# Small products of the HGRN heads and the state-space branch, cut in pieces and placed between the k steps of the projections

## The chip, the cores and the metric

The kernel runs on one core of one Trainium2 chip. The metric is the device time of one execution in microseconds, the median of several runs. Half a dozen engines work side by side: TensorE (matrix products; its weight loads are listed apart), VectorE, ScalarE, GpSimd, and SyncE, which only issues transfers. Transfers run on DMA engines.

## The reference, cut to what matters

The program is two transformer-like blocks on a sequence of 512 tokens and 1024 features, in float32. The change lies in the mixer of the second block, where 16 extra tokens stand ahead of the sequence (528 in all):

```
p   = rmsnorm(h) @ w_in                       # 1024 -> 7 x 1024
y_a = s5_mixer(p[:, :1024])                   # state-space branch: 64 groups of 16
y_b = hgrn2_mixer(q, f, i, og)                # p[:, 1024:5120]: 8 heads of 128
out = sigmoid(g1) * (y_a @ Wa) + sigmoid(g2) * (y_b @ Wb)      # gates: p[:, 5120:]

# one HGRN head, chunk by chunk:
#   o     = mask(q_in @ k_in.T) @ v + q_in @ state
#   state = decay * state + k_out.T @ v
#   o     = rmsnorm(o) * g * silu(og)
# state-space branch: states by a linear recurrence over time, y = C @ states + D * u
```

## The kernel before, in words

Every large product is done in three passes (`mm3`, lines 122 to 128): both operands are split into a high and a low part, and high x high, high x low and low x high are summed in one PSUM bank. A projection of the second block is `prod2` (line 1110): 128 output features of all tokens, in two column ranges of 264 or 258 tokens, eight k steps for each; a k step is the three passes of one 128-row slice of the contraction. So a projection has 16 k steps, 48 products on TensorE, and it fills a PSUM tile of two banks, of which there are two. The small products take PSUM tiles of one bank (`aux`), of which there are four. Weights come through landing buffers (`raw`, line 86: two, and a third one in this stage, in turn), are split by ScalarE and VectorE (lines 131, 132) into one of three slots, and stay there until their products are done.

The stage of this document runs from about 866 to 1302.8 us. Head by head (`head`, line 1250) come four projections: forget gate f, output gate og, input i, query q, and between them long chains on ScalarE and VectorE that make the scaled keys (line 1297 the last of them) and queries (line 1303). The back half of a head is small products in plain float32, which appear as two records each: transposes of i and of the output keys (1311, 1315); the scores within chunks, 4 x 4 products with 32 streamed columns each (1328) and one for the extra tokens (1334); the key-value products for the states (1339, 1341); the outputs (1351, 1352, 1354); and, after a norm on VectorE (1365), transposes back (1371, 1373).

The state-space branch has three parts. Its input is written to DRAM and read back in another layout as U (line 1175). `s5_state` makes the driving terms in eleven groups of small products with 64 by 66 columns (1195), then runs the recurrence on VectorE, 64 dependent steps of four instructions (1206 to 1209). `s5_out` rearranges the states on ScalarE (1216), then makes the outputs in ten groups of up to seven (1228, 1229; 66 columns), each group with its own loaded matrices (1224), then a gelu (1232), and y goes to DRAM (1234) and is read back (1426) for the gated output.

`gates` (line 1385) are 16 more projections after the eight heads, with a sigmoid and a store of each by GpSimd (1395).

What sets the order: the functions are generators, and a loop (from line 1398) steps through them by hand, one head's projections in turn with the former head's back half and, from head 4 on, a group of state-space outputs. That is the order of tracing. A planner in the language's layer then orders each engine's instructions by its own estimate of when they are ready; among those that are ready, the one traced first goes first. Once planned the order of an engine is fixed, and each engine works in that order; so does each queue that issues transfers (SyncE for the loads, GpSimd for most stores).

Of the kernel before, what the change touches and what calls it, by code (L numbers as in the profile page):

```python
# [69 lines left out]
class Kern:  # L70
# [15 lines left out]
    def raw(self):  # L86
        """The next landing place of a weight load."""
        self.nraw += 1
        if self.xraw is not None and self.nraw % 3 == 2:
            return self.xraw.tile([P, WCAP], F32, tag="xraw", bufs=1, name=self.nm("xraw"))  # L90
        return self.wpool.tile([P, WCAP], F32, tag="wraw", bufs=self.wbufs[0], name=self.nm("wraw"))
# [12 lines left out]
    def split_w(self, H, L, raw, sz):  # L104
        """H, L <- the two parts of raw, in two pieces so that neither engine is held for long."""
        h = sz // 2
        for a, b in ((0, h), (h, sz)):
            self.split(H[:, a:b], L[:, a:b], raw[:, a:b])

    def load_w2(self, srcs, kt, n):  # L110
        """Several [kt*128, n] blocks in one weight slot."""
# [28 lines left out]
    def rsqrt_act(self, out, ss, n, tag):  # L140
        """out <- (ss / n + EPS) ** -0.5: square root, reciprocal, one Newton step."""
# [11 lines left out]
    def rsqrt_dve(self, out, ss, n, tag):  # L153
        """out <- (ss / n + EPS) ** -0.5 by a bit estimate and three Newton steps."""
# [14 lines left out]
    def later(self, lag, fn):  # L169
        """Queue fn to be traced after the next lag products."""  # L170
# [96 lines left out]
    def ada_tiles(self, c0, n, dst, acc):  # L267
        """dst <- columns c0.. of silu(c) @ w_ada + b_ada, one column per 128; a generator of its steps."""
# [16 lines left out]
    def bcast_rows(self, dst, rstd, n):  # L285
        """dst [P, n*128] <- rstd[:, t] of token t*128+p, on every partition."""
# [8 lines left out]
    def sumsq_add(self, kt, acc, sq, x, e=None):  # L295
        """acc <- acc + x * x, feature tile by feature tile."""
# [7 lines left out]
    def sumsq_rows(self, ps, acc, t0, sizes):  # L304
        """Per token sums over the partitions of acc: column t0 + i of ps for the i-th token tile."""
# [5 lines left out]
    def rstd_rows(self, ps, cols, rb):  # L311
        """rb, on every partition: the reciprocal roots of the mean squares of the tokens in cols; ps: their sums of squares."""
# [17 lines left out]
    def scale_split(self, H, L, x, g):  # L330
        """H, L <- the two parts of x * g, g per partition."""
# [3 lines left out]
    def modulate(self, tiles, src, rb, G, sh, H, L):  # L335
        """H, L <- the two parts of src * rb * G + sh, feature tile by feature tile."""
# [52 lines left out]
    def rope(self, out, x, key, t, heads, rstd):  # L389
        """out, x: [P, heads, d] views; rstd [P, heads]."""  # L390
# [13 lines left out]
    def scores(self, qT, kT, mask):  # L404
        """qT, kT: [d, 512] (scaled). Softmax rows of the four query tiles."""
# [22 lines left out]
    def probs_T(self, probs):  # L428
        """Per key tile j: the probabilities of queries j*128.., keys on the partitions."""
# [21 lines left out]
    def block1(self):  # L451
        nc, tc, A = self.nc, self.tc, self.A
        V = self.V = {}
        with ExitStack() as es:
            b1 = es.enter_context(tc.tile_pool(name="b1", bufs=1, reuse_waits="tile"))
            # x in, its transpose, and the first modulation columns
# [8 lines left out]
            with tc.tile_pool(name="b1x", bufs=1, reuse_waits="tile") as xp:  # L465
# [6 lines left out]
                # silu(c) @ w_ada for the first shift and scale: the last rows on the tensor engine  # L472
# [63 lines left out]
            # latents  # L536
# [56 lines left out]
            # MLA q: 2 x 4 heads of 96  # L593
# [33 lines left out]
            # MLA k, v: 2 x 4 heads of 128  # L627
# [29 lines left out]
            # dilated q, k, v  # L657
# [34 lines left out]
            # attention  # L692
# [60 lines left out]
            for kh in range(2):  # L753
                if kh:
                    # x2 * G2 for the first products, which run before the token norms are known
# [34 lines left out]
        # FFN  # L790
# [100 lines left out]
    def expm1_parts(self, pool, x, parts, n):  # L891
        """2^k and expm1(r) with x = k ln2 + r."""
# [82 lines left out]
    def s5_poles_T(self):  # L975
        """The poles' powers with the states on the partitions, in both halves."""
# [133 lines left out]
    def prod2(self, W, fs, src, ranges, nk=KD):  # L1110
        """T-layout product: PSUM [P, 2, 512]; ranges: two (start, n) column ranges of src."""
        ps = self.psP.tile([P, 2, 512], F32, tag="pp", bufs=2, name=self.nm("pp"))
        for a, (c0, n) in enumerate(ranges):
            for kt in range(nk):
                self.mm3(ps[:, a, :n], (W[0][:, kt, fs], W[1][:, kt, fs]), (src[0][:, kt, c0 : c0 + n], src[1][:, kt, c0 : c0 + n]), kt == 0, kt == nk - 1)
        return ps[:, :, : ranges[0][1]]

    def block2(self):
# [17 lines left out]
        # hgrn lower bounds: softmax over the two rows, first row  # L1136
# [42 lines left out]
        def s5_state():  # L1179
            nonlocal Hs  # L1180
            v_ = slot(2).rearrange("p a b -> p (a b)").rearrange("p (c r g) -> p c r g", c=66, r=2)
            for c0 in range(0, 32, 3):
# [13 lines left out]
                nc.scalar.copy(v_[:, :, :, c0 : c0 + n].rearrange("p c r g -> p r g c"), p4)  # L1196
            self.tap("v", v_)
# [13 lines left out]
        def s5_out():  # L1211
# [8 lines left out]
            for g0 in range(0, 64, 7):  # L1220
                yield
                n = min(7, 64 - g0)
                MO = self.raw().rearrange("p (g s x) -> p g s x", s=2, x=P)
                nc.sync.dma_start(MO[:, :n].rearrange("p g s x -> p g (s x)"), self.MO_d[:, g0 : g0 + n])
                ps = self.aux()
                for i in range(n):
                    o = ps[:, i * 66 : i * 66 + 66]
# [22 lines left out]
        def head(hd, Ws, fs):  # L1250
# [6 lines left out]
            yield  # L1257
# [4 lines left out]
            yield  # L1262
# [42 lines left out]
            Q1, QI = E1, E3  # L1305
            yield
            # token-layout v and k_out
            def tok(src, s):
                pt_ = self.aux()
                for c in range(NT):  # L1310
                    nc.tensor.transpose(pt_[:, c * P : c * P + P], ch(src)[:, c], self.ident)
                o = T(s, 1, (P, NT, P))
# [5 lines left out]
                return o, om  # L1318
            VT, VM = tok(I, "VT")
            KT, KM = tok(KO, "KT")  # L1320
# [3 lines left out]
            for c in range(NT):  # L1324
                for i in range(4):
                    n = 32 * (i + 1)
                    lhs = KX[i][:, c] if i else ch(K1)[:, c, :32]
                    nc.tensor.matmul(p3[:n, c, 32 * i : 32 * i + 32], lhsT=lhs, rhs=ch(Q1)[:, c, 32 * i : 32 * i + 32], start=True, stop=True)  # L1328
            for i in range(4):
# [6 lines left out]
            # states before each chunk  # L1336
# [3 lines left out]
            for c in range(3):  # L1340
# [305 lines left out]
```

## Time and profile before

| | |
|---|---|
| median of 3 runs | 1876.71 us (1876.2 to 1882.28) |
| the profiled execution, first to last instruction (span) | 1874.8 us |
| TensorE busy, share of the span | 96% |
| VectorE | 58% |
| ScalarE | 42% |
| GpSimd | 17% |
| stage of the heads and gates | 866 to 1302.8 us |

The profiled execution's own time is known by its span alone, 1.9 us under the median of the runs. A busy TensorE is not TensorE at its peak: products are pipelined, and the clock it is granted can be at either of two levels; a row of a stretch gives the mean as PEclk. In rows of the timeline the second number is how long one record lasted (for several records together, from the first's start to the last's end); what a product costs is the distance from one start to the next.

### The profile page before, as it was taken

To read this page: it belongs to the slowest core of one execution; us is meant where nothing else is said; L and a number is where in the kernel's file an instruction comes from. 1 tells how busy PE (TensorE), PEld (TensorE's weight loads), DVE (VectorE), ACT (ScalarE), POOL (GpSimd) and SP (SyncE) were. 2 spreads that over 40 slices of the span, in tenths; PEclk is the share of its full clock that TensorE was granted. 3 is DMA by queue.
4 is the path that set the end of the run, shared out by engine and by line. 5 is a ranking of instruction groups with operands and counts; after the bars stand their busy time and mean duration, and the time that the engine had idled before them with its cause. 6 is when DMAs were issued, how large, how long until landed. Compare 5 with 4: busy or idle time off the path is not lost. (4 is left out here: it accounts for less than half of the span.)

```text
span 1874.8 us, 28652 instructions
## 1 busy us (share of the span) xinstructions
PE 1796.3 (96%) x11605; PEld 1570.5 (84%) x11605; DVE 1079.9 (58%) x2281; ACT 785.1 (42%) x1290; POOL 320.8 (17%) x440
## 2 busy tenths in 40 slices
PE   1989999999999999999799999999999999999998
PEld 1777765787777777889799999999999999989996
DVE  5697857787543465554488334442444476536652
ACT  3674555345432343333545645342322444324432
POOL 5000000058763861012000000110000000000001
PEclk9899999999999999999899899999999999999999
DMA  7332524343334335355722244824643322332231
GB/s 272 107 111 93 187 91 135 110 78 125 96 112 124 129 116 155 112 188 99 185 74 91 71 135 150 183 97 160 216 139 113 102 91 68 102 107 95 69 102 45
DMA packets 178767, 226.66 MB, mean 121 GB/s; under 512 B 10699, under 2 KB 146746, under 8 KB 175178
## 3 DMA queue, kind: packets, MB, share of 16 engines
q1 hardware_dynamic: 164256, 181.95, 30.6%
q0 software_dynamic: 10640, 38.19, 7.6%
q10 hardware_dynamic: 3738, 4.69, 0.7%
q8 instruction: 91, 1.49, 0.3%
q14 instruction: 42, 0.34, 0.1%
HBM read 196.29 MB, written 32.70 MB: 122 GB/s over the span
## 5 line engine op out<-in xcount | busy, mean ns | idle before, releaser
L126 PE MATMUL pp<-s,wh 128*128 128x258 f32 (+2 forms) x1856 | 533.2, 287 | 2.3 <-DVE st L1206 1.0
L127 PE MATMUL pp<-s,wh 128*128 128x258 f32 (+2 forms) x1856 | 531.6, 286 | 0.0
L128 PE MATMUL pp<-s,wl 128*128 128x258 f32 (+2 forms) x1856 | 529.4, 285 | 0.0
L132 DVE TENSOR_TENSOR wl<-wraw,wh 128x1024 fp32r<-128x1024 f32 (+4 forms) x264 | 307.6, 1178 | 193.8 <-ACT wh L131 192.8
L131 ACT CAST wh<-wraw 128x1024 fp32r<-128x1024 f32 (+4 forms) x264 | 249.1, 965 | 365.9 <-PE pp L127 232.4
L126 PEld LDWEIGHTS pp<-s,wh 128*128 128x128 f32 x1856 | 355.9, 192 | 5.1 <-issue 1.6
L127 PEld LDWEIGHTS pp<-s,wh 128*128 128x128 f32 x1856 | 356.6, 192 | 0.3 <-DVE s L333 0.2
L128 PEld LDWEIGHTS pp<-s,wl 128*128 128x128 f32 x1856 | 356.5, 192 | 0.0
L126 PE MATMUL pp<-h2H,wh 128*128 128x512 f32 x336 | 134.2, 400 | 2.4 <-DVE cy L852 2.4
L127 PE MATMUL pp<-h2L,wh 128*128 128x512 f32 x336 | 133.8, 398 | 0.8 <-DVE h2L L343 0.7
L128 PE MATMUL pp<-h2H,wl 128*128 128x512 f32 x336 | 132.6, 395 | 0.0
L126 PEld LDWEIGHTS pp<-h2H,wh 128*128 128x128 f32 x336 | 63.4, 189 | 20.2 <-ACT aH L131 2.8
L127 PEld LDWEIGHTS pp<-h2L,wh 128*128 128x128 f32 x336 | 63.4, 189 | 16.0 <-DVE h2L L343 2.0
L128 PEld LDWEIGHTS pp<-h2H,wl 128*128 128x128 f32 x336 | 63.6, 189 | 14.4
L126 PE MATMUL pp<-aH,wh 128*128 128x512 f32 x176 | 70.1, 398 | 0.0
L127 PE MATMUL pp<-aL,wh 128*128 128x512 f32 x176 | 69.8, 396 | 0.0
L128 PE MATMUL pp<-aH,wl 128*128 128x512 f32 x176 | 69.8, 396 | 0.0
L1563 POOL TENSOR_TENSOR ht<-ht,gf 128x512 f32<-128x512 f32 x4 | 5.7, 1434 | 344.7 <-ACT fsq L1561 344.7
L126 PE MATMUL pp<-wh,hH 128*128 128x512 f32 (+1 forms) x160 | 62.7, 392 | 1.2 <-ACT hH L519 1.2
L127 PE MATMUL pp<-wl,hH 128*128 128x512 f32 (+1 forms) x160 | 62.2, 388 | 0.5 <-DVE wl L132 0.5
L1527 DVE TENSOR_TENSOR xz<-pp,rb_f 128x516 f32<-128x516 f32 x44 | 30.6, 696 | 54.3 <-PE pp L128 54.3
L128 PE MATMUL pp<-wh,hL 128*128 128x512 f32 (+1 forms) x160 | 61.5, 385 | 0.0
(598 smaller groups left out, 3566.1 us busy)
## 6 DMA issues: line engine op xcount, KB each, us to landing
wraw<-in_w_up_dram SPq DMA_DIRECT2D x40, 1024.0 KB, 5.8
wada<-in_w_ada_dram SPq DMA_DIRECT2D x24, 1024.0 KB, 5.0
wraw<-in_w_in_dram SPq DMA_DIRECT2D x17, 1024.0 KB, 6.0
wraw<-in_w_in_dram SPq DMA_DIRECT2D x26, 512.0 KB, 6.3
wraw<-in_w_down_dram SPq DMA_DIRECT2D x16, 704.0 KB, 4.5
wraw<-in_w_down_dram SPq DMA_DIRECT2D x8, 1024.0 KB
xraw<-MO_d SPq DMA_DIRECT2D x5, 896.0 KB
sg_d<-sg POOLq DMA_DIRECT2D x16, 258.0 KB, 2.4
```

The source lines that it names most:

```text
L126: mm(ps, lhsT=sh, rhs=mh, start=start, stop=False)
L127: mm(ps, lhsT=sh, rhs=ml, start=False, stop=False)
L128: mm(ps, lhsT=sl, rhs=mh, start=False, stop=stop)
L131: self.nc.scalar.copy(H, x)
L132: self.nc.vector.tensor_tensor(L, x, H.bitcast(F32), ALU.subtract)
L1527: nc.vector.tensor_tensor(xz, ps, rb, ALU.mult)
L1563: nc.gpsimd.tensor_tensor(h, h, gf[:, :512], ALU.mult)
```

## The change

`prod2` calls a new function, `slot`, behind each of its k steps. `slot` counts, and calls the next step of each generator in a list (`fillers`), at each slot or at each second one. The head's projections are traced in one go, and its back half becomes a generator of its own (`back`), cut by yields into pieces of about two products; it is handed to the next head's k steps as a filler. The state products follow as fillers of head 1, at each slot; the state-space outputs as fillers from head 5 on, at each second slot, each group's matrices being requested eight calls before their products. What is left of a head's back half at the end of the next head is traced there (`flush`). Comments and docstrings go too.

```diff
+    def slot(self):
+        self.nslot += 1
+        for f in list(self.fillers):
+            if self.nslot % f[1] == 0 and next(f[0], self) is self:
+                self.fillers.remove(f)
+
+    def flush(self, gen):
+        for f in list(self.fillers):
+            if f[0] is gen:
+                self.fillers.remove(f)
+        for _ in gen:
+            pass
...
                 self.mm3(ps[:, a, :n], ..., kt == 0, kt == nk - 1)
+                self.slot()
...
         # s5_state, after each of the eleven groups
                 nc.scalar.copy(v_[:, :, :, c0 : c0 + n]..., p4)
+                yield
...
         # s5_out
             for g0 in range(0, 64, 7):
-                yield
...
                 nc.sync.dma_start(MO[:, :n]..., self.MO_d[:, g0 : g0 + n])
+                for _ in range(8):
+                    yield
                 ps = self.aux()
                 for i in range(n):
+                    if i % 2 == 0:
+                        yield
...
         # head: the yields between its projections go
+            return back(hd, I, KO, K1, KX, E1, E3, dec, og)
+
+        def back(hd, I, KO, K1, KX, Q1, QI, dec, og):
...
                 for c in range(NT):
                     nc.tensor.transpose(...)
+                    if c % 2:
+                        yield
...
             for c in range(NT):
                 for i in range(4):
                     ...                                     # a score product
+                    if i % 2:
+                        yield
...
             vec.copy_predicated(SM, ...)
+            yield
...
             for c in range(3):
+                yield
                 nc.tensor.matmul(s3[:, c + 1], lhsT=KT[:, c], rhs=VT[:, c], start=True, stop=True)
...
-            yield
+            for _ in range(3):
+                yield
...
             for c in range(NT):
                 ...                                         # two output products
+                yield
...
             vec.tensor_scalar(onm, pm[:4, :P], rs[:4, 4:5], None, ALU.mult)
-            yield
+            for _ in range(16):
+                yield
...
-        s5 = iter(())
-        prev = iter(())
+        prev, s5 = iter(()), iter(())
         for hd in range(9):
+            self.fillers = [[prev, 1], [s5, 1 if hd == 1 else 2]]
             if hd < 8:
...
             else:
-                cur = gates()
-            for g in (cur, prev, cur, prev, cur, prev):
-                next(g, None)
-                if g is cur:
-                    next(s5, None)
+                cur = iter(())
+                gates()
+            self.flush(prev)
             prev = cur
             if hd == 0:
-                s5_state()
-            if hd == 4:
+                s5 = s5_state()
+            elif hd == 1:
+                self.flush(s5)
+            elif hd == 4:
                 s5 = s5_out()
-                next(s5, None)
-            next(s5, None)
-        for _ in cur:
-            pass
+        self.flush(s5)
+        self.fillers = []
```

## Rows read from the trace of the kernel before

**Rows 1.** The page: the span, and the engines' busy time, share and instructions.
```profile
span 1874.8 us, 28652 instructions
PE 1796.3 (96%) x11605; PEld 1570.5 (84%) x11605; DVE 1079.9 (58%) x2281; ACT 785.1 (42%) x1290; POOL 320.8 (17%) x440
```

**Rows 2.** Stretches of the stage: length, busy time by engine, granted clock, DMA.
```profile
core 0: us, PE busy (x) PEld busy (x) DVE busy (x) ACT busy (x) POOL busy (x), PEclk, DMA share, GB/s
889.60:911.00 21.40, 10.90 (x260) 10.57 (x260) 1.29 (x2) 7.71 (x11) 0.00 (x0) 0.76 0.67 147
911.00:1049.20 138.20, 137.21 (x1063) 130.96 (x1061) 110.87 (x458) 84.53 (x112) 3.51 (x7) 0.94 0.34 97
1049.20:1107.70 58.50, 56.46 (x414) 54.00 (x412) 25.30 (x58) 24.92 (x35) 1.86 (x4) 0.85 0.34 107
1107.70:1190.60 82.90, 82.44 (x652) 79.46 (x651) 38.80 (x98) 42.98 (x61) 7.46 (x11) 0.94 0.60 150
1190.60:1302.80 112.20, 108.47 (x865) 106.58 (x865) 37.84 (x57) 39.20 (x52) 11.77 (x21) 0.95 0.43 141
1302.80:1874.80 572.00, 563.94 (x4211) 538.35 (x4209) 299.02 (x376) 191.25 (x257) 9.03 (x9) 1.00 0.33 107
```

**Rows 3.** Short stretches, same view: scores, behind them, state-space outputs, a long fall.
```profile
1024.40:1029.40 5.00, 5.00 (x45) 4.30 (x43) 1.88 (x10) 4.60 (x3) 0.22 (x1) 1.00 0.59 184
1029.50:1032.90 3.40, 3.40 (x19) 3.40 (x18) 3.24 (x11) 3.39 (x2) 0.00 (x0) 0.50 0.00 0
1049.80:1053.30 3.50, 3.48 (x31) 3.32 (x30) 1.46 (x2) 2.93 (x3) 0.00 (x0) 1.00 0.01 2
1063.60:1080.70 17.10, 17.10 (x86) 15.71 (x85) 4.49 (x17) 6.55 (x12) 0.00 (x0) 0.50 0.16 55
```

**Rows 4.** Timeline of TensorE, one head: start, duration, line, operation, shapes, count.
```profile
1024.26 0.28 PE L128 MATMUL pp<-s,wl 128*128 128x258 f32 x1
1024.46 0.25 PE L1328 MATMUL aux<-E,LM 128*32 128x32 f32 x2
...
1025.38 0.25 PE L1328 MATMUL aux<-E,LM 128*32 128x32 f32 x2
...
1028.27 0.48 PE L1339 MATMUL aux<-VTm,KTm 16*128 16x128 f32 x2
1028.69 0.94 PE L1341 MATMUL aux<-VT,KT 128*128 128x128 f32 x6
1029.38 0.46 PE L126 MATMUL pp<-s,wh 128*128 128x258 f32 x1
...
1029.85 0.42 PE L128 MATMUL pp<-s,wl 128*128 128x258 f32 x1
...
1032.43 0.42 PE L128 MATMUL pp<-s,wl 128*128 128x258 f32 x1
...
1033.02 0.28 PE L128 MATMUL pp<-s,wl 128*128 128x258 f32 x1
...
1035.18 0.28 PE L128 MATMUL pp<-s,wl 128*128 128x258 f32 x1
1035.30 0.39 PE L1351 MATMUL aux<-VT,ST 128*128 128x128 f32 x2
```

**Rows 5.** TensorE's waits from 815 to 1310 us: total, times, longest.
```profile
PE aux L1195 <- DMA U<-u_d: 8.4, 1, 8.4
PE aux L1371 <- DVE KT L1365: 2.7, 1, 2.7
PE aux L1228 <- DMA xraw<-MO_d: 2.5, 2, 2.0
```

**Rows 6.** Timeline of VectorE, one head: the last scaled key, the scaled queries.
```profile
1012.78 0.68 DVE L1297 TENSOR_TENSOR KX<-LM,RD 128x512 f32<-128x512 f32 x1
...
1016.79 0.68 DVE L1303 TENSOR_TENSOR E<-pp,E 128x516 f32<-128x516 f32 x1
```

**Rows 7.** Timeline of GpSimd's queue: y's stores, its reload.
```profile
1170.41 6.09 POOL L1234 DMA_DIRECT2D y_d<-s  x8 [13.91 <-ACT s L1232]
...
1204.77 0.91 POOL L1426 DMA_DIRECT2D yT<-y_d  x1
```

More of the change, by code (lines that the diff above doesn't have):

```diff
@@ L1304, in head, with tok @@
             vec.tensor_tensor(q2(E3), psq, q2(E3), ALU.mult)
-            Q1, QI = E1, E3
-            yield
-            def tok(src, s):
+            return back(hd, I, KO, K1, KX, E1, E3, dec, og)
+        def back(hd, I, KO, K1, KX, Q1, QI, dec, og):
+            T = lambda s, b=1, shp=(P, L2): hp.tile(list(shp), F32, tag=s, bufs=b, name=self.nm(s))
+            vec = nc.vector
+            def tok(src, s, out):
                 pt_ = self.aux()
@@ L1317, in tok @@
                 nc.scalar.copy(om, pm[:META, :P])
-                return o, om
-            VT, VM = tok(I, "VT")
-            KT, KM = tok(KO, "KT")
+                out += [o, om]
+            VK = []
+            yield from tok(I, "VT", VK)
+            yield from tok(KO, "KT", VK)
+            VT, VM, KT, KM = VK
             ST, SM = STs[hd % 2], STm[hd % 2]
@@ L1345, in head @@
                 vec.scalar_tensor_tensor(Sx[:, c + 1], Sx[:, c], dec[:, c + 1 : c + 2], s3[:, c + 1], ALU.mult, ALU.add)
-            yield
+            for _ in range(3):
+                yield
             po = self.aux()
@@ L1367, in head @@
             vec.tensor_scalar(onm, pm[:4, :P], rs[:4, 4:5], None, ALU.mult)
-            yield
+            for _ in range(16):
+                yield
             pt_ = self.aux()
@@ L1395, in gates @@
                         nc.gpsimd.dma_start(sg_d[gi, :, f, 12:], sg[:, 12:])
-                    yield
-        s5 = iter(())
-        prev = iter(())
+        prev, s5 = iter(()), iter(())
         for hd in range(9):
+            self.fillers = [[prev, 1], [s5, 1 if hd == 1 else 2]]
             if hd < 8:
@@ L1595, in run @@
             self.queue = []
+            self.fillers, self.nslot = [], 0
             self.act_norm = (2, 3)
```

## Prediction

> **What bounds the kernel now.** I read the page's busy shares first, then the stretches of the trace with their granted clock, then TensorE's own order of work around one drop of the clock, then TensorE's waits, and last single rows of VectorE and GpSimd.
>
> The page says TensorE: 96% busy, the next engine 58% [rows 1]. So only TensorE's own work, its clock and its few waits can move the end. The stretches show where that work is not at full pace. From 1302.8 us to the end the granted clock is 1.00; in the stage that the change touches it is 0.94, 0.85, 0.94 and 0.95 [rows 2]. The clock has two levels, 1.00 (2.4 GHz) and 0.50 (1.2 GHz), so a mean of 0.94 over 138.2 us is 2 x 0.06 x 138.2 = 16.6 us at the low level. The four stretches give 16.6 + 17.6 + 9.9 + 11.2 = 55 us at half clock, some 3.5 us of them near 1244 us behind a wait of line 1371 [rows 5], so 52 us in eight falls, one for each head.
>
> What stands ahead of a fall is plain in one head. From 1024.40 to 1029.40 TensorE was busy all the time with nothing but small products, the clock still at 1.00; from 1029.50 to 1032.90 it ran at 0.50 on ordinary k steps [rows 3]. In the order of work [rows 4] the block is the 16 score products of line 1328 (32 columns streamed each), four rounds of 0.92 us (1024.46 to 1025.38 is the first), then lines 1334, 1339 and 1341: 4.9 us without one projection. Every head has this block once, and the low level comes at its end. Not every block of small products does it: 3.50 us of state-space outputs alone, at 1049.80, ran at 1.00 [rows 3], and what is unlike them in the scores is how little is streamed per product.
>
> The price of the low level is in the same rows: from 1029.85 to 1032.43 twelve products of a k step take 2.58 us, 0.215 each; from 1033.02 to 1035.18 eighteen take 2.16, 0.120 each. Half clock loses 1 - 0.120/0.215 = 44% of its time on projections, a little less on small products bound by weight loads; I use 43%: 52 x 0.43 = 22.4 us lost.
>
> **The change part by part.** Durations are those of the profiled execution, span 1874.8 us; the median of the runs is 1876.7, so 1.9 us lie around the span, and I carry the difference over to the median unchanged.
>
> *Scores between k steps.* No product is added or removed. The back half of a head becomes 40 steps, one behind each k step of the next head's first products (64 slots); a step with scores holds two of the 16 products, 0.92/2 = 0.46 us [rows 4], beside a k step of 3 x 0.120 = 0.36 us. So for 8 slots 44% of TensorE's time is projections, where now there are none for 4.9 us. The trace before has no such mixture at this ratio; bounds for the clock are all falls kept (0) and all gone (-22.4). The nearest row is the 3.50 us of state-space outputs at 1.00 [rows 3], denser than the scores alone, as the mixture is. I take nine tenths: -20.2 us. The tenth left is for a head in which steps bunch, because the scheduler issues what its own estimate calls ready, and late queries release several steps at once.
>
> *Switching.* The runs of small products per head go from about five to 23 (4 transposes, 8 scores, 6 for states, 4 outputs and one more, 1 final), 18 x 8 = 144 more; the state-space outputs go from 10 blocks to 37 pieces, +27, the state products from one block to 11, +10: 181 more interruptions of the projections. Price of one: from 0 (a projection at 1035.18, the output product at 1035.30, 0.12 us as between projections; small to projection likewise behind line 1341) up to 0.19 us (line 1339, 16 rows high: 1028.27 to 1028.69 is 0.42 us where two of line 1341 take 0.23) [rows 4]. For the score pairs the switch into 32 columns, 0.20 us at 1024.46 instead of 0.12, is paid inside the block too, at each round. So I take 0 for full-width pieces and two dear switches for lines 1334 and 1339: 8 x 0.4 = 3.2; 10 state pieces of 64 columns at 0.15, 1.5. Together +5; bounds 0 and 181 x 0.19 = 34.
>
> *State-space loads.* A group's matrices are now requested 16 slots before their products. The waits on them, 2.5 us in two [rows 5], should go: -2 (bounds 0 and -2.5). They share the landing buffers with the head's weights, in SP's order; those have a whole head, over 30 us, to arrive.
>
> *State products in head 1.* Their first piece stands now behind one k step and two transposes instead of right behind head 0. The wait for U, 8.4 us [rows 5], is a DMA's and stays, as does the low clock around it (0.76 over 889.6 to 911, [rows 2]); 0 (bounds +1, and -10 if the scheduler puts head 1's first products ahead of it).
>
> *Waits that TensorE may now meet.* A small piece that is late holds every projection queued behind it. Scores start four slots into the next head, 2.5 us behind the query product, where six more microseconds lie between now. In one head the last scaled key is done at 1013.46 and the queries at 1017.47 [rows 6], the query product itself having ended about 1015.1 (by 96 products of i and q at 0.122 behind the outputs that end at 1003.3); so scores would be wanted about as the queries get ready. The final transposes follow the outputs by 16 slots, some 7 us; the one wait of this kind now is 2.7 us [rows 5]. I take +3 for all eight heads; bounds -2.7 (the present one gone) and +16 (2 us a head).
>
> *Tail.* The state-space outputs run at one call in two slots: 119 calls, 238 slots, of which heads 5 to 7 have 192; the end, with its gelu, moves about 47 slots into the gates. Those 47 slots hold 17 us of k steps and 15 us of small work, so y goes out near 1205 instead of 1170.41 [rows 7]. Hidden: the reload of y was issued at 1204.77 [rows 7], 98 us ahead of the gated output, which starts where the stage ends, at 1302.8 [rows 2]; with y 35 us later and the stage's end 14 us earlier, 49 us are left for the reload and its splits. If that cover were gone, each microsecond late would count whole. GpSimd's queue takes the reload's wait, and the stores of the gates behind it: 0, bounds 0 and +10.
>
> Sum: -20.2 + 5 - 2 + 0 + 3 + 0 = -14.2; 1876.7 - 14.2 = 1862.5, say 1862 us.
>
> **The rivals.**
>
> *Switching is dear (slower).* Place: each entry and exit of a small piece, weights not loaded ahead. At the upper price 34 us against 20.2 - 2 gained and 3 new: 1876.7 + 34 - 19.2 = about 1892. It decides from (20.2 + 2 - 3)/181 = 0.106 us a piece. For: the row of line 1339. Against: full-width neighbours switch free [rows 4]. Chance 0.06.
>
> *Falls stay, by bunching.* If the queries come late in the scheduler's estimate, most steps of a head become ready together and go out as a block again. For: they get ready just when wanted [rows 6]. Against: eight steps must bunch, and they are released by one thing only 2 us late. Falls kept in half of the heads: 1862 + 10 = 1872. Chance 0.12.
>
> *Falls stay, by another cause.* If idle time and not thin work took the clock down, spreading products would change nothing: 1876.7 + 5 - 2 + 3 = 1883. Against: TensorE was busy 5.00 of 5.00 us ahead of the fall [rows 3]. Chance 0.03. The Trainium skill's page "TensorE: Matmul & The Clock Gate", section "HAM oscillation — how this bites in real kernels", names TensorE's idle gaps between bursts as what brings the low clock; by that rule the eight falls, which have no gap ahead of them, would be left as they are. The trace disagrees for seven of them and agrees for the one at 1063.6 us, where a wait on a load stood ahead.
>
> *The tail bites.* GpSimd waiting for y holds the gates' stores, their buffers fill, TensorE stops: +10, 1872. Chance 0.07.
>
> *More is won.* Head 1's projections fill the wait for U: 1862 - 10 = 1852. Chance 0.08.
>
> **How the numbers follow.** The forecast has 0.64, with a range of its own from 1853 to 1871. What a measurement of this kernel can tell from no change is about 0.3%, 5.6 us: faster is below 1871, slower above 1882. Faster: nearly all of 0.64, the 0.08, and about 0.04 of the cases around 1872: 0.76. Same: most of the cases at 1872: 0.13. Slower: dear switching, the other cause, some of bunching with all its costs: 0.11. For 8 in 10 the range goes from 1849, below the case at 1852, to 1877, which leaves out dear switching and the other cause.
>
> **What would show it.** Right: a granted clock of 1.00 nearly throughout from the end of the state products to the gates, line 1328 in pairs of products with three projections between, the waits on the state-space loads gone, projections at 0.12 us apart on both sides of a piece. Wrong: rows of 0.50 that still follow each head's scores; gaps of 0.2 us at each change of product; new waits of the lines 1328, 1352 or 1371 on VectorE; or a wait of the gated output on y.

## The result, and the profile after

Five runs of the changed kernel take 1890.4 us (1887.6 to 1894.0), five of the kernel before on the same chip 1876.2 (1867.6 to 1882.3): 1.0081 times the time before, 95% interval 1.0059 to 1.0104. It is slower, by some 14 us, where 14 faster were forecast.

First the page after (span; busy time, share and instructions by engine), which answers to [rows 1]:

```profile
span 1889.9 us, 28637 instructions
PE 1789.1 (95%) x11605; PEld 1559.6 (83%) x11605; DVE 1077.3 (57%) x2281; ACT 779.0 (41%) x1286; POOL 321.7 (17%) x440
```

The same products in as many instructions, 7 us less busy time, and a span 15 us longer: TensorE stands still for longer, by 22 us. The stretches of the stage, with the columns of [rows 2], say where:

```profile
889.60:916.00 26.40, 26.40 (x255) 26.03 (x254) 2.98 (x5) 7.32 (x9) 0.00 (x0) 1.00 0.41 56
916.00:1054.50 138.50, 123.61 (x1114) 114.13 (x1113) 108.79 (x458) 78.47 (x110) 4.60 (x9) 0.95 0.37 110
1054.50:1106.40 51.90, 46.33 (x328) 43.56 (x329) 19.76 (x51) 23.71 (x34) 1.08 (x2) 0.80 0.23 69
1106.40:1198.80 92.40, 92.40 (x763) 87.41 (x761) 40.04 (x107) 37.17 (x58) 2.18 (x4) 1.00 0.35 109
1198.80:1317.00 118.20, 98.95 (x801) 97.78 (x800) 36.06 (x48) 43.66 (x51) 16.75 (x27) 0.91 0.63 164
1317.00:1889.90 572.90, 564.87 (x4212) 539.29 (x4210) 299.12 (x376) 191.40 (x257) 9.06 (x10) 1.00 0.33 107
```

The remainder is as long as before, 573 us against 572. All of the loss lies in the stage, which ends at 1317.0 and not at 1302.8: 14.2 us. And yet 92.4 us in the middle of it now run with TensorE busy throughout at 1.00, where before no stretch of the stage had more than 0.95. So the change did part of what it was to do. What went against it is in TensorE's waits over the stage (total, times, longest), beside [rows 5]:

```profile
PE pp L126 <- ACT sg L1428: 19.2, 3, 17.5
PE pp L126 <- DVE s L1226: 10.7, 1, 10.7
PE aux L1355 <- ACT VT L1337: 7.8, 1, 7.8
PE aux L1405 <- DVE KT L1398: 1.4, 4, 0.5
...
PE pp L128 <- DVE wl L132: 0.5, 1, 0.5
```

That is 39.6 us, against 17.6 before (the three rows of [rows 5] and 4.0 us in three smaller ones). Of the waits of [rows 5], those on U and on the matrices of the state-space outputs have gone, and that of the final transposes (line 1371 before, 1405 now) is down from 2.7 to 1.4 us. Three long ones have come, each in one place. The stage has three falls left, and each begins inside one of these three waits (the columns are again those of the stretches):

```profile
935.10:948.80 13.70, 5.29 (x22) 4.78 (x23) 12.66 (x53) 4.16 (x6) 0.00 (x0) 0.50 0.19 53
1054.60:1075.10 20.50, 15.49 (x72) 13.73 (x72) 1.61 (x7) 7.60 (x8) 0.00 (x0) 0.50 0.00 0
1238.90:1259.40 20.50, 6.08 (x28) 6.08 (x29) 0.30 (x1) 1.21 (x2) 2.00 (x3) 0.50 1.02 218
```

TensorE works for 26.9 us at half clock here, the second number of each row together. Before it was the prediction's 55 us and 5.1 more in the fall at U's wait, which the prediction left out of its count:

```profile
893.00:903.20 10.20, 5.10 (x93) 5.13 (x95) 0.00 (x0) 2.52 (x3) 0.00 (x0) 0.50 0.35 45
```

At the prediction's 43% the difference, 33.2 us, gives back 14 us. Waits +22, half clock -14, and some +6 left over (the stage's 14.2 less these two). The trace says what the 6 us are: summed over all products at full clock, from start to start, projections take 15.5 us more beyond 0.12 us each than before, and small products 9.7 less; these are the changes between small and wide products.

No fall follows scores alone any more. In the middle of a head a pair of scores stands between k steps, and the clock stays at 1.00 (first TensorE's timeline, then that stretch in the view of the stretches):

```profile
984.66 0.28 PE L128 MATMUL pp<-s,wl 128*128 128x264 f32 x1
984.87 0.25 PE L1355 MATMUL aux<-E,LM 128*32 128x32 f32 x2
985.05 0.30 PE L1355 MATMUL aux<-E,KX 128*64 128x32 f32 x2
985.28 0.40 PE L126 MATMUL pp<-s,wh 128*128 128x264 f32 x1
985.52 0.29 PE L127 MATMUL pp<-s,wh 128*128 128x264 f32 x1
```

```profile
981.00:986.00 5.00, 5.00 (x45) 4.52 (x43) 5.00 (x19) 4.28 (x8) 1.08 (x2) 1.00 0.20 78
```

The first projection behind a pair holds TensorE for 0.24 us (985.28 to 985.52) and not the usual 0.12. That alone is not yet a price, because the last small product ahead of a projection can be shorter than its like inside a block. Here is a piece of full width, two transposes:

```profile
980.50 0.38 PE L1333 MATMUL aux<-ident,I 128*128 128x128 f32 x2
980.63 0.37 PE L126 MATMUL pp<-s,wh 128*128 128x264 f32 x1
980.84 0.28 PE L127 MATMUL pp<-s,wh 128*128 128x264 f32 x1
```

From 980.50 to 980.84 it is 0.34 us, what two transposes at 0.11 and one projection at 0.12 take without any change of width: the projection takes 0.21, but the transposes only 0.13 together. So full-width pieces are free, as the prediction had it. A piece of scores is not, quite: over 36 of them at full clock it is 0.76 us from the start of the projection ahead to that of the second projection behind, against 0.70 by the rates of [rows 4], 0.06 us each.

Now the three waits, each by what makes it.

*Gates.* GpSimd's queue after, and below it ScalarE's next sigmoid; the last bracket says how long the engine stood idle and for what:

```profile
1222.42 6.09 POOL L1254 DMA_DIRECT2D y_d<-s  x8 [4.95 <-ACT s L1252]
1229.24 0.57 POOL L1429 DMA_DIRECT2D sg_d<-sg  x1 [0.73 <-DMA y_d<-s]
1234.66 0.56 POOL L1429 DMA_DIRECT2D sg_d<-sg  x1 [4.85 <-DMA y_d<-s]
1252.65 0.91 POOL L1457 DMA_DIRECT2D yT<-y_d  x1 [17.43 <-DMA y_d<-s]
1253.56 0.55 POOL L1429 DMA_DIRECT2D sg_d<-sg  x1
```

```profile
1252.67 0.60 ACT L1428 ACTIVATE sg<-pp 128x516 f32<-128x516 f32 x1 [14.91 <-DMA sg_d<-sg]
```

The stores of y go out at 1222.42, 52 us later than in [rows 7] (17 later than forecast), and so among the gates. Two stores of gates, of the sigmoids at 1223.44, follow them on the same queue, at 1229.24 and 1234.66. How long these two take from issue to landing:

```profile
L1429 POOL DMA_DIRECT2D sg_d<-sg x2: 557/564/572, 1229.2 to 1234.7; - x2
DMA to landing us min/median/max: 18.8/21.1/23.3
```

The usual time is 2.3 to 2.7 us. They land at 1252.6 and 1253.4, right behind the last of y's eight stores (1252.0). From 1229.3 to 1252.6 the DMA engines are busy all the time (DMA share 1.02), at 140 GB/s where it was 329 just before (1218 to 1222). The gates have two buffers, and both are held by these two stores, so ScalarE, and then TensorE, stops until the first has landed.

The planner put y's reload between the gates' stores, as before; there y had long been written, here the reload waits 17.4 us at the head of the queue. But it is issued behind the two stores (1252.65), so it can't be what holds them: it waits for the same stores of y as they do, and only the gates' stores from 1253.56 on stand behind it.

*Copies.* ScalarE's timeline around 1050 us:

```profile
1042.88 8.00 ACT L1233 COPY s<-s 64x2080 f32<-64x2080 f32 x2
...
1051.54 7.40 ACT L1233 COPY s<-s 64x2080 f32<-64x2080 f32 x2
1058.97 0.59 ACT L1337 COPY VT<-aux 128x512 f32<-128x512 f32 x1
```

The four copies of the states, 15.4 us together, are ready before the transposed values of head 4 and go first; the scores of that head and the projections behind them wait for `VT` until 1059.6.

*Head 1.* VectorE's scan of head 1 (line 1286):

```profile
918.48 1.26 DVE L1286 TENSOR_TENSOR_SCAN Lc<-rst,F 128x528 f32<-128x528 f32 x1 [14.67 <-PE aux L1339]
...
942.19 0.69 DVE L1322 TENSOR_TENSOR E<-pp,E 128x516 f32<-128x516 f32 x1
```

TensorE's wait is put down to line 1226, an operation of the states' recurrence, but what TensorE needs is the end of head 1's vector work, and that starts late. The planner put all four projections of head 1 first, which covers U, then the state products, and the transposes of head 0 among them. Head 1's scan writes the buffer that those transposes still read, so VectorE stands idle for 14.7 us ahead of it, the queries are scaled at 942.19, and TensorE waits for a product buffer until 943.0.

### The profile page after: what moved, and what is told of

Read it like the earlier page. It is cut to its first block, busy times and chain, and to the rows that moved or that the text cites. A ratio compares the mean times of both kernels' runs of the same rounds, so it can differ in the third digit from the quotient of the medians.

```text
span 1889.9 us, 28637 instructions
## 1 busy us (share of the span) xinstructions
PE 1789.1 (95%) x11605; PEld 1559.6 (83%) x11605; DVE 1077.3 (57%) x2281; ACT 779.0 (41%) x1286; POOL 321.7 (17%) x440
## 4 chain that ended last, share of the span: by engine, by line
PE 75%; issue 12%; DVE 6%; DMA 4%; ACT 2%; POOL 1%; ACTq 0%; POOLq 0%; DVEq 0%
PE pp L126 18%; PE pp L127 17%; PE pp L128 17%; PE pp L411 2%; PE pv L449 2%; PE aux L1355 1%; DMA sg_d<-sg 1%; DVE wl L132 1%; PE pd L126 1%; PE pd L128 1%; PE pd L127 1%; PE aux L1078 1%; PE aux L438 1%; PE aux L127 1%; PE aux L128 1%
## 5 line engine op out<-in xcount | busy, mean ns | idle before, releaser
L126 PE MATMUL pp<-s,wh 128*128 128x258 f32 (+2 forms) x1856 | 544.5, 294 | 30.4 <-ACT sg L1428 19.2
L132 DVE TENSOR_TENSOR wl<-wraw,wh 128x1024 fp32r<-128x1024 f32 (+4 forms) x260 | 302.8, 1178 | 168.5 <-ACT wh L131 167.6
L131 ACT CAST wh<-wraw 128x1024 fp32r<-128x1024 f32 (+4 forms) x260 | 244.9, 964 | 341.2 <-PE pp L127 217.8
L126 PEld LDWEIGHTS pp<-h2H,wh 128*128 128x128 f32 x336 | 63.5, 189 | 20.2 <-ACT aH L131 2.8
## 6 DMA issues: line engine op xcount, KB each, us to landing
wraw<-in_w_in_dram SPq DMA_DIRECT2D x17, 1024.0 KB, 13.6
```

The costliest lines, as they stand in the source:

```text
L126: mm(ps, lhsT=sh, rhs=mh, start=start, stop=False)
L131: self.nc.scalar.copy(H, x)
L132: self.nc.vector.tensor_tensor(L, x, H.bitcast(F32), ALU.subtract)
```

## The experiments

All edits are to the changed kernel; line numbers shift by up to 3. Times are medians, ratios against runs of the kernel before on the same chip; where two experiments ran on different chips, compare the ratios. Waits and falls are read from one profiled execution of each kernel.

**1. The heads alone in pieces.**

```diff
# s5_state: no yield between groups; s5_out: one yield a group
-            self.fillers = [[prev, 1], [s5, 1 if hd == 1 else 2]]
+            self.fillers = [[prev, 1], [s5, 16]]
...
             if hd == 0:
-                s5 = s5_state()
+                self.flush(s5_state())
             elif hd == 4:
                 s5 = s5_out()
+                next(s5)
+                next(s5)
```

> The heads' back halves stay cut in pieces; the state-space branch goes back to the order of the kernel before (state products in one block between heads 0 and 1, copies and the first output group at the end of head 4, ten output groups in one block each, four to a head). Three-waits theory (the loss is three waits that the state-space pieces make: 17.5 us of the gates on a store, 7.8 us of the scores on the copies, 10.7 us in head 1, each with a half clock behind it): the gates' 22 us and the copies' part go, the wait for U and its half clock come back for the 13 us of head 1, so 1860 to 1868 us, well under the kernel before; the heads' falls stay away. Rival, cutting itself is dear (each change between wide and small products costs much more than in the trace): over 1880 us, with no wait in the gates. Rival, the clock part won nothing: 1874 to 1880 us.

1866.4 us against 1874.4, ratio 0.9947 (0.9925 to 0.9969): as the three-waits theory had it. U's wait is back (9.2 us), and no fall follows scores without a wait. Cutting the heads gains; the loss came with the state-space branch.

**2. Output groups at every step**, so that y is done within head 7.

```diff
-            self.fillers = [[prev, 1], [s5, 1 if hd == 1 else 2]]
+            self.fillers = [[prev, 1], [s5, 1]]
```

> The changed kernel with a state-space piece at every step of the projections in place of every second, so that the last output group is done within head 7 and its stores stand well ahead of the gates on GpSimd's queue. Three-waits theory: the 17.5 us wait of the gates and the half clock behind it go, the other two waits stay: 1868 to 1874 us, the remainder as before. Rival, the reload of y is late because the stores of y are slow wherever they stand: the wait in the gates stays or goes elsewhere on TensorE, 1885 us or more. Rival, denser pieces cost in the heads what the tail gives back: 1880 to 1890 us.

1882.8 us, 1.0040 (1.0024 to 1.0056): in the range of the third theory alone. The wait in the gates fell from 17.5 to 3.0 us, but gelu now stands ahead of `VT` on ScalarE in head 7, a new fall of 13.6 us came there, and the one behind the copies grew from 20.5 to 27.3.

**3. The copies in 16**, two at each of the eight empty steps.

```diff
-            for par in range(2):
-                for r in range(2):
-                    nc.scalar.copy(SS[64 * r : 64 * r + 64, par::2, 1:], ...)
...
                 for _ in range(8):
+                    for g, par, r in pieces[:2]:    # 8 groups of a quarter
+                        nc.scalar.copy(SS[64 * r : 64 * r + 64, 2 * g + par : 2 * g + 16 : 2, 1:], ...)
+                    pieces = pieces[2:]
                     yield
```

> The changed kernel with the four copies of the states (3.9 us each on ScalarE) cut into 16, two at each of the eight empty steps ahead of the first output group, behind the load of its matrices. Three-waits theory: the 7.8 us wait of the scores for the copy of the transposed values and the half clock behind it (some 6 us) go, the other two waits stay: 1875 to 1880 us. Rival, the scores of that head wait for something else (the load of the matrices, or VectorE) and the copies only happen to stand there: 1887 to 1892 us, the wait under another name.

1889.6 us, 1.0080 (1.0056 to 1.0104), the wait still 5.0 us. A failure of the edit: the planner still put ten of the pieces, 11 us, ahead of `VT`. Tracing order only decides among what its estimate calls ready. The run says nothing on the theory.

**4. The state products one head later.**

```diff
-            self.fillers = [[prev, 1], [s5, 1 if hd == 1 else 2]]
+            self.fillers = [[prev, 1], [s5, 1 if hd == 2 else 2]]
...
-            if hd == 0:
+            if hd == 1:
                 s5 = s5_state()
-            elif hd == 1:
+            elif hd == 2:
                 self.flush(s5)
```

> The changed kernel with the state products at the steps of head 2 in place of head 1, so that no piece of them stands between the transposes of head 0. Three-waits theory: head 0's transposes go in head 1's first steps, its scan waits no longer (14.7 us now), and the 10.7 us wait of TensorE for a product buffer goes while the wait for U stays covered: 1875 to 1880 us. Rival, the state scan of 256 small VectorE operations holds head 1's queries up (the page names it as the releaser): the same wait comes one head later, 1887 to 1892 us.

1885.3 us, 1.0050 (1.0031 to 1.0070), and the wait came one head later, 10.6 us, so my expectation fell. But the picture came whole: all of head 2's projections first, then state products with head 1's transposes among them, and VectorE's scan idle for the same time on the same thing:

```profile
951.94 1.26 DVE L1286 TENSOR_TENSOR_SCAN Lc<-rst,F 128x528 f32<-128x528 f32 x1 [14.67 <-PE aux L1339]
```

U cannot be the cause here; the state products' place among the transposes, or their scan, can. Experiment 7 tells these apart.

**5. The gates' stores on ScalarE's queue.**

```diff
-                        nc.gpsimd.dma_start(sg_d[gi, :, f, 12:], sg[:, 12:])
+                        nc.scalar.dma_start(sg_d[gi, :, f, 12:], sg[:, 12:])
```

> The changed kernel with the 16 stores of the gates issued from ScalarE's queue in place of GpSimd's, where the reload of y stays; nothing of the order of the pieces is changed. If GpSimd's queue is the cause (the reload waits 17.4 us at its head and the gates' stores stand behind it): the 17.5 us wait of the gates and the half clock behind it go while the stores of y and the reload come as late as before, 1868 to 1873 us. Rival, the transfers themselves are slow there (the eight scattered stores of y fill the DMA engines): the gates' buffers come free as late as before, 1886 us or more.

1886.5 us, 1.0073 (1.0056 to 1.0090), by the time alone the rival's range. TensorE's waits in that kernel, and the two sigmoids of the place:

```profile
PE pp L126 <- ACT sg L1428: 5.1, 3, 3.4
PE pp L126 <- ACT s L1462: 3.5, 1, 3.5
```

```profile
1237.58 0.60 ACT L1428 ACTIVATE sg<-pp 128x516 f32<-128x516 f32 x1 [8.19 <-DMA sg_d<-sg]
1245.10 0.60 ACT L1428 ACTIVATE sg<-pp 128x516 f32<-128x516 f32 x1 [5.41 <-DMA sg_d<-sg]
```

Sharing the queue with y's stores was the larger part of the cause: TensorE's waits on the gates' sigmoids fall from 19.2 to 5.1 us, and the last gate's sigmoid starts at 1300.3, after it did at 1315.6. The rival has the rest: on a queue of their own the two stores, issued from 1223.1 on, still hold the next sigmoids until 1237.6 and 1245.1, while y's stores run as long as before. (The run doesn't tell y's stores from the reload's wait, since the gates' stores get away from both; the order of issue in the trace of the changed kernel does.) But ScalarE then has all eight casts of y in one run behind the last gate:

```profile
1301.77 8.60 ACT L1462 CAST s<-yT 128x528 fp32r<-128x528 f32 x8
1315.36 0.61 ACT L1473 ACTIVATE sgl<-pp 128x520 f32<-128x520 f32 x1 [4.99 <-PE pp L128]
```

The gated output waits for them, a fall of 10.2 us follows, and its first sigmoid comes at 1315.4, after it did at 1320.5. Of 15 us won 10 are given back.

**6. The copies on GpSimd** (`nc.gpsimd.tensor_copy` for `nc.scalar.copy`).

> The changed kernel with the four copies of the states on GpSimd, not on ScalarE. The cut into 16 pieces left ten of them ahead of the copy of the transposed values, so it did not test the theory. If ScalarE's order is the cause: the transposed values are copied as soon as they are there, the 7.8 us wait of the scores and the 20.5 us of half clock behind it go, unless the first output group now waits for GpSimd: 1874 to 1880 us. Rival (the scores wait for something else at that place): 1888 to 1892 us.

1889.3 us, 1.0087 (1.0068 to 1.0106), by the time alone the rival's. The scores wait for `VT` no longer, but a wait of 10.4 us has come under another name. GpSimd's copies, VectorE's timeline beside them, and TensorE's wait of that place:

```profile
1035.76 16.23 POOL L1233 COPY s<-s 64x2080 f32<-64x2080 f32 x4
```

```profile
1035.69 0.68 DVE L1280 TENSOR_TENSOR og<-og,pp 128x516 f32<-128x516 f32 x1
1036.29 3.43 DVE L166 SCALAR_TENSOR_TENSOR rs<-nwt,rs 128x5 f32<-128x5 f32 x1
```

```profile
PE aux L1405 <- DVE KT L1398: 10.4, 1, 10.4
```

Operations of 5 columns, 0.15 us elsewhere, last nearly as long as one of GpSimd's copies (3.7 to 4.7 us). The edit exchanged one wait for another, so its time decides nothing on the copies; the next run does.

**7. The state products behind the back half** of head 0.

```diff
         def s5_state():
             nonlocal Hs
+            for _ in range(40):
+                yield
```

> The changed kernel with 40 empty steps ahead of the first state product, so that all pieces of head 0's back half come before it in the order of tracing. Two theories are left for the 10.7 us wait in head 1. (a) The state products between the transposes hold head 0's back half back until U is there, and head 1's scan, which needs the buffer of those transposes, starts 14.7 us late: the wait goes but for some 3 us for head 2's weights, which are loaded behind the matrices of the states: 1877 to 1883 us. (b) The state scan's 256 small operations stand between head 1's vector work whatever comes before it: the wait of about 10 us stays, 1887 to 1892 us.

1881.1 us, 1.0036 (1.0014 to 1.0058), in the range of (a). The 10.7 us wait has gone, as (a) had it and against (b). But what it paid is little: the state products stand as a block behind head 1 and bring waits of 3.0 us (on their matrices) and 2.8 (on head 2's weights) and 10.2 us of half clock, and the last of head 3's final transposes starts at 1040.9, after 1041.9. The time comes from the next head. The state scan, later too, ends behind head 4's transposes, and so do the copies on ScalarE:

```profile
1046.61 0.59 ACT L1339 COPY VT<-aux 128x512 f32<-128x512 f32 x1 [0.82 <-PE aux L1335]
...
1052.18 15.29 ACT L1235 COPY s<-s 64x2080 f32<-64x2080 f32 x4 [3.56 <-DVE s L1228]
```

The scores wait no longer, an output group waits 3.4 us in their place, and from head 3's to head 4's final transposes it is 38.5 us, not 48.3, with 15 projections fewer in the stretch (some 2 us); to head 7's, where this has evened out, it is 162.6, not 171.7. What differs in that head is the order of the copies, and of the recurrence ahead of them. So by this trace the order costs some 9 us; no run shows it with nothing else changed, since the edits of experiments 3 and 6 missed.

**8. Heads alone, state products in one block behind head 1** (in experiment 1, `if hd == 1: self.flush(s5_state())`).

> The heads' back halves alone in pieces, as in the first experiment (1866.4 us), with the state products in one block behind head 1's projections in place of head 0's. By theory (a) head 1's projections cover U (9.2 us of wait and the half clock behind it there), and head 0's back half runs in head 1's first steps: 1848 to 1858 us, the best version so far. By theory (b), or if the loads of head 2's weights, which now stand behind those of the state matrices, come late by as much as U did: 1863 to 1870 us.

1862.0 us, 0.9936 (0.9914 to 0.9957): between the forecasts of (a) and (b), so it decides nothing between them. It is better than experiment 1 by 4 us by the medians and 2 by the ratios, whose intervals overlap.

**9. Experiments 2 and 7 together.**

> The changed kernel with both edits that moved it: 40 empty steps ahead of the first state product (1881.1 us alone) and a state-space piece at every step (1882.8 us alone); all pieces stay cut. If the three waits are the loss, the edits add: the gates' wait falls from 17.9 to about 3 us and its half clock goes, so 1868 to 1875 us, under the kernel before. Rival, cutting the state-space branch costs by itself: 1877 us or more, with no long wait left to name.

1866.1 us, 0.9960 (0.9935 to 0.9986): 2 us under its forecast, and with all pieces still cut the kernel is under the one before. The longest wait left is 3.3 us. Cutting the state-space branch is not dear in itself.

**10. Experiment 8, the first output group a quarter of a head later** (one `next(s5)` less).

> The heads' back halves in pieces, state products in one block behind head 1's projections (1862.0 us), and now the first output group a quarter of a head later, behind the copies of the states. If the 3.5 us wait of that group for the copies and the 6.9 us of half clock behind it were the last loss in head 5: 1854 to 1859 us. Rival, it only moves: 1860 to 1864 us.

1859.7 us, 0.9920 (0.9888 to 0.9952), the lowest median of all. The wait that it was to remove is still 3.2 us and its fall 10.2, so the rival was right on the wait; the 2 us against experiment 8 are within the spread of the runs.

**11. Experiment 10 with the scores in one block** (the yield behind every second score goes).

> The kernel of the run before it with the 16 score products of a head in one block again, all other pieces cut. If the falls of the clock follow thin products in a row while TensorE is busy, they come back behind the scores of seven or eight heads, 3.4 to 6.8 us of half clock each, and the seven changes between wide and narrow products that go in each head give back 2 us: 10 to 20 us slower than that kernel. Rival, the falls follow waits only: no fall behind scores that are not waited for, the same time within 3 us or faster by the 2 us.

1863.9 us, 0.9941 (0.9919 to 0.9963): 4 us slower than experiment 10, less than forecast, and the intervals overlap. The traces decide. One head's score block and what follows, as stretches:

```profile
1045.70:1050.70 5.00, 5.00 (x46) 4.32 (x44) 4.52 (x12) 1.45 (x4) 0.00 (x0) 1.00 0.01 3
1050.70:1057.50 6.80, 6.80 (x31) 6.26 (x31) 2.18 (x12) 5.09 (x2) 0.22 (x1) 0.50 0.41 135
```

TensorE is busy in every one of the 5.00 us ahead of the fall. Five heads have such a fall of 6.8 us. Experiment 10 has none: its four falls each have a wait of 2.1 to 3.2 us ahead. So thin products in a row do take the clock down without a wait, in five heads of eight, not in all. In sum TensorE works for 44.4 us at half clock here and 23.6 in experiment 10; at the prediction's 43% that is 9 us, of which the 56 changes of width that go, at 0.06 us, give back 3.

**12. Experiment 10 with the scores alone in pieces** (transposes, states and outputs in blocks).

> The same kernel with the scores in pieces of two and the rest of each back half (transposes, chunk states, outputs) in blocks. If the score block alone brings the clock down: within 3 us of the kernel with all pieces, no falls behind scores, and fewer changes of width. If the products of states and outputs in a row do it too: falls of 3.4 us behind them in most heads, 5 to 12 us slower.

1860.6 us, 0.9926 (0.9900 to 0.9952), the same as experiment 10, and no fall without a wait ahead. Of all the pieces of a head only the scores need cutting.

**13. Experiment 10 with a late tail.**

```diff
             for g0 in range(0, 64, 7):
-                yield
+                for _ in range(7 if g0 == 63 else 1):
+                    yield
```

> The kernel with the heads alone in pieces (1859.7 us) with one thing added: the last state-space output group 96 steps later, so that the last product, gelu and the stores of y fall among the first gates as in the changed kernel. If a late y costs by itself what the trace of the changed kernel shows (17.5 us of wait in the gates, some 1 us of other gate waits, and a fall of 20.5 us of half clock of which little work falls in it): 15 to 25 us slower, 1875 to 1885 us, with the reload waiting some 17 us at the head of GpSimd's queue. By the prediction's account (49 us are left, so the tail costs 0 to 10): 1860 to 1870 us.

1873.1 us, 0.9984 (0.9971 to 0.9997), 13 us more than experiment 10 (12 by the two ratios). Its GpSimd queue and TensorE's wait:

```profile
1242.15 0.91 POOL L1454 DMA_DIRECT2D yT<-y_d  x1 [17.05 <-DMA y_d<-s]
```

```profile
PE pp L126 <- ACT sg L1426: 13.7, 1, 13.7
```

It is the same wait at the same place. Here too two gate stores, issued at 1218.86 and 1224.54 and so ahead of the reload, land 23.2 and 18.4 us later, behind y's. The tail alone costs 12 to 13 us, a little under the forecast of 15 to 25.

## Why the prediction was wrong

It forecast -14.2 us; the stage came out +14.2. Two steps failed, the tail and the waits that TensorE may meet. By its own steps:

- *Tail, costed at 0*: **the step that failed most.** It counted the reload's own slack ("49 us are left for the reload") and found it ample, which it was, and gave the danger half a sentence without a price of its own ("GpSimd's queue takes the reload's wait, and the stores of the gates behind it: 0, bounds 0 and +10"). The queue, the gates' stores and their buffers are the right ones; what holds the stores is not the reload but the transfers of y's own stores. The chain y's stores, two gate stores behind them, two buffers, ScalarE, TensorE measures 18.3 us of added wait (19.2 against 0.9), and 12 to 13 us of time by itself in experiment 13. The rival "the tail bites" had the chain but for what starts it, at +10 and a chance of 0.07.
- *Scores between k steps, -20.2*: right in kind. The falls behind scores all went, and experiment 11 brought five of them back. What is left of the gain is -12 (-14 with U's fall), because new waits took the clock down again: 26.9 us of work at half clock are left, 15.5 of them behind the copies.
- *Waits that TensorE may now meet, +3*: **the second step that failed.** The places named (scores wanted about when the queries are ready, final transposes) cost less than before, 1.4 us against 2.7. The wait that came, 7.8 us, was at a place that it did not look at: the four copies, which the change moved by a fraction of a head on ScalarE, ahead of `VT`. With the half clock behind it this is some 9 us (experiment 7).
- *State products in head 1, 0*: the sum holds, the reason doesn't. U's wait of 8.4 us went (the rival "more is won"), and 10.7 us of another kind took its place, with as much work at half clock as before (5.3 us against 5.1).
- *Switching, +5*: right, +6 by the starts in the trace, and right in that full-width pieces are free. What it left out are the 0.06 us of each of the 64 score pieces.
- *State-space loads, -2*: right; no wait on them is left.

With the long waits out and all pieces still cut, experiment 9 is at 0.9960 of the kernel before, 1869 us on the prediction's scale: 7 above the forecast and inside its range. So the gain that it priced is there; what it missed is what moved work does to the queues beside TensorE.

The rival by which only idle time takes the clock down is refuted by experiment 11, but not without a point. The Trainium skill, "TensorE: Matmul & The Clock Gate", section "HAM oscillation — how this bites in real kernels", blames gaps in TensorE's work; the three falls of the changed kernel (at 935, 1055 and 1239 us) each have one ahead, of 7.8 to 17.5 us, and agree; the five falls of experiment 11 have none, and disagree. In the kernel before, the prediction counted one of eight falls with a wait ahead; it is two, that of head 0 at 916.9 us too (waits of 1.6 and 0.95 us ahead), and the one at 1063.6 begins before its head's scores (1067.9). Six are left that follow a score block with no wait over 0.5 us near, three of 3.4 us and three of 6.8.

The balance by name is not exact: the tail's 12 to 13 us come from one edit to another kernel than the changed one, the copies' 9 from a stretch of a trace; together they make up some 22 of the 28 us between forecast and result. The rest was not pulled apart.

## What to carry to other kernels

When work is moved later, follow not only its consumer's slack but what will stand behind it in its queue: eight stores that nobody needs for some 50 us stopped TensorE for 17.5, because two stores that free buffers had to land behind them. Spread thin products between wide ones for the clock's sake, but only those whose inputs wait for nothing that the same move has shifted; here cutting the 16 score products of each head gave some 4 us (at the edge of the noise, but with five falls of the clock gone in the trace), and the rest of the cutting changed nothing or cost. Where a planner orders by its own estimate of readiness, a step moved in the source moves other steps too: read the planned order of each engine's neighbours, not of the moved step alone.

## What the runs showed of the hardware

- Float32 copies on GpSimd hold up VectorE: four copies of 64x2080 in 16.23 us made VectorE operations of 128x5, 0.15 us elsewhere, last 3.43 to 3.60 us, while two with an operand in PSUM kept their usual 0.69 and 0.33 us inside the fourth copy (lines 1398 and 1400). The Trainium skill, "SBUF — State Buffer", section "SBUF: two separate sides", has the two engines exclude each other from a shared port for a whole instruction where VectorE reads two operands from SBUF; the rows agree in both cases. An operation on one SBUF tensor (line 1305, 128x16) was held in the fourth copy too, 2.94 us in place of 0.23, which that condition doesn't explain.
- A block of 16 score products brought a fall of 6.8 us in five heads of eight (experiment 11), none in the other three; in the kernel before, six such blocks with no wait near brought three falls of 3.4 us and three of 6.8: the same work, not always the same fall.
- Going from small products back to projections of 264 columns, the first projection takes 0.20 to 0.24 us from its start to the next, not 0.12. Behind products of full width the last of these is as much shorter (0.03 us in place of 0.11), so the change costs nothing; a pair of score products of 32 columns loses 0.06 us.
- Two stores of 258 KB, issued on GpSimd's queue behind eight of 264 KB that fill the DMA engines (share 1.02), landed 18.8 and 23.3 us after their issue, where 2.3 to 2.7 is usual; from ScalarE's queue they still held their buffers for some 14 and 21 us beside the same eight (experiment 5).
